# Storing output tile 58 as 104 + 24 rows instead of 100 + 28 rows

## The chip, the cores and the metric

The kernel runs on one core of one Trainium2 chip. The metric is the device time of one execution in microseconds (us). Before the change the median of the first three runs was 210.65 us (210.45 to 210.84).

## The reference

```python
batch, m, k, n = 16, 512, 1024, 768            # all float32
def reference(x, weight, bias, residual):
    return (np.matmul(x, weight) + bias + residual).astype(np.float32)
```

That is 8192 rows of 1024 numbers times a 1024x768 matrix. With `x` and the residual read and the output written, the core moves 87 MB.

## The kernel before

The 8192 rows are 64 tiles of 128 rows, in four superblocks S of 16 tiles. All loads and stores are issued on SyncE's queue in the fixed order of a list, `ORDER`. An entry `('s', S, j0, j1)` stores tiles `16*S+j0` to `16*S+j1-1`; a further number cuts the store's 128 partitions at that row into two stores. The end of the list is:

```python
ORDER = [ ...                                      # loads and earlier stores cut here
 ('r', 3, 7, 16), ('s', 2, 0, 16), ('s', 3, 0, 10), ('s', 3, 10, 11, 100), ('s', 3, 11, 13),
 ('s', 3, 13, 14), ('s', 3, 14, 15), ('c', 3, 15, 0), ('c', 3, 15, 1)]
LAST = [(0, 512), (512, 256)]                      # columns of the two stores of tile 63
```

So the program ends with these stores: ten tiles in one (48 to 57), tile 58 cut at row 100, tiles 59 and 60 in one, then 61, 62, and tile 63 in two column pieces. The issuing code is:

```python
n0, nl = (0, N) if kind == "s" else LAST[j1]
j1 = j1 if kind == "s" else j0 + 1
edges = [0, *cut, P]                               # P = 128
for p0, p1 in zip(edges, edges[1:]):
    K_(nc.sync.dma_start(
        out=out_d[S, p0:p1, j0:j1, n0:n0 + nl],
        in_=R[p0:p1, (J * S + j0) % RR:(J * S + j0) % RR + j1 - j0, n0:n0 + nl],
    ))
```

By the Trainium skill ("DMA: Bandwidth & Descriptors", section "Why a DMA increments its semaphore by 16 and not by 1"), a DMA issued from SyncE uses the largest k up to 16 that divides its number of rows, on the lowest-numbered k engines, and each of them increments the semaphore when its own share has landed. The trace agrees on k: the 100-row store has 10 completions, the 28-row store 14, and whole tiles have 16. Tile 58 is 128 rows of 3072 bytes, so the cut at 100 gives engines 0-9 ten rows and then two more, engines 10-13 two rows, and engines 14 and 15 none.

## Time and profile before

| | before |
|---|---|
| median of the first three runs | 210.65 us |
| span of the profiled run (its time: 210.74 us) | 209.0 us |
| end of the last vector add | 204.50 us |
| first and last of the 16 landings of the last store | 206.20 and 207.88 us |

From the page of before: busy time of TensorE, the tenths of busy time of PE and DMA in 40 slices of the span, and the DMA queues.

```profile
span 209.0 us, 3115 instructions
PE 201.5 (96%) x1298; PEld 130.0 (62%) x1298; DVE 104.7 (50%) x140; ACT 66.2 (32%) x69; POOL 115.9 (55%) x72
...
PE   7899999999999999999999999999999999999990
...
DMA  6999999999989899999999999999999999998984
...
q1 hardware_dynamic: 4912, 87.05, 97.9%
q8 instruction: 10, 0.16, 0.3%
```

TensorE and the DMA engines are both busy nearly all the time. For the tail the question is what ends last. From the chain that ended last, restricted to 201 us and later (start, duration, what):

```profile
200.79 0.65 PE psum_o L164 x4
201.44 2.61 PE psum_o L258 x16
204.05 0.02 issue
204.08 0.42 DVE ro L262
```

The computing is over at 204.50 us, 4.5 us before the span ends. From the waits of SyncE's queue from 190 us on (who waited for whom: us in total, times, longest):

```profile
SPq L292 <- DMA out_dram<-ro: 3.0, 1, 3.0
```

So the end is a wait for stores. From the table of stretches of before (stretch, its length, the busy time of the five engines, granted clock, DMA share, GB/s):

```profile
205.00:205.50 0.50, 0.00 (x0) 0.00 (x0) 0.00 (x0) 0.00 (x0) 0.00 (x0) 1.00 1.00 389
205.50:206.00 0.50, 0.00 (x0) 0.00 (x0) 0.00 (x0) 0.00 (x0) 0.00 (x0) 1.00 0.90 334
206.00:206.50 0.50, 0.00 (x0) 0.00 (x0) 0.00 (x0) 0.00 (x0) 0.00 (x0) 0.62 0.42 162
206.50:207.00 0.50, 0.00 (x0) 0.00 (x0) 0.00 (x0) 0.00 (x0) 0.00 (x0) 0.50 0.32 117
207.00:207.50 0.50, 0.00 (x0) 0.00 (x0) 0.00 (x0) 0.00 (x0) 0.00 (x0) 0.50 0.14 49
207.50:208.00 0.50, 0.00 (x0) 0.00 (x0) 0.00 (x0) 0.00 (x0) 0.00 (x0) 0.50 0.00 0
```

The second-to-last number is the one to read. The share is 1.00 while all 16 engines work, and then it falls, to 0.90, 0.42, 0.32 and 0.14. The engines do not finish together; a few carry a backlog. (A packet counts in the stretch in which it starts, and the last landing comes 0.34 us after the end of the last packet. So the share is 0.00 after 207.50 us although landings follow until 207.88.) The semaphore records of the trace say how many. The 16 landings of the last store (issued at 204.53 us), in us:

```
206.20 206.21 206.24 206.25 206.28 206.30 206.31 206.34 206.38 | 206.65 207.07 207.14 207.38 207.50 207.83 207.88
```

Nine engines land about 1.7 us after the issue. That is the latency of a small store on an idle engine. The other seven are still busy with earlier stores.

Two further readings need the packet records of the trace (start, duration and size of every DMA packet, without the engine's number). On one engine the next packet starts 3 or 4 ns before the previous one ends, and the sequence of sizes is known from `ORDER`. So the packets can be chained into 16 sequences, one for each engine. Where two engines start packets of the same size within about 2 ns the chains may be swapped; the packets of tile 58 show which group of engines a chain belongs to. A 3072-byte packet takes 121 ns and the next one starts 118 ns after it, so **one row of tile 58 costs its engine 0.118 us**.

The ten packets of queue 8 are instruction fetches of 16 KB each. The Trainium skill ("Runtime: NRT & Kernel Launch", section "Instruction fetch mechanics") says that instructions are refilled in 16 KiB blocks of 256. TensorE's 2 x 1298 instructions make just over ten such blocks, which agrees with the ten packets. That the fetches are TensorE's rests on this count; the trace does not name their engine. Each fetch sits in one engine's chain, between its data packets. This is one engine of 10-13 in the trace of before (start us, ns, bytes):

```
174.350  1029  27648
175.375  1033  27648
176.405  1098  16384   <- instruction fetch
177.488  1493  27648   <- the next packet takes 0.46 us longer as well
178.978     9      4   <- its completion
```

This engine loses about 1.55 us to the fetch: 1.08 us from the fetch's start to the next packet's, and 0.46 us in that packet. The fetch at 196.4 us does the same to an engine of 14-15, which loses 1.42 us (1.04 + 0.39). These two hits fall just before the end and are not made up for: at the end of the ten-tile store these two engines were at 202.57 and 202.40 us and all others between 198.8 and 201.1. Without the 1.55 us the first would have been near 201.0. That the fetches are the cause rests on this sum.

### The profile page before, as it was taken

Reading aid. Unit: us, or ns where it says so; the run is one execution under the profiler, and the core shown is the slowest. Engines: PE = TensorE matmul, PEld = TensorE weight load, DVE = VectorE, ACT = ScalarE, POOL = GpSimd, SP = SyncE. Lnnn points to the kernel's source line nnn. Section 1 sums busy time; section 2 is a strip of 40 time slices with the busy share of each in tenths; the row PEclk is TensorE's granted clock in tenths of the full one; section 3 lists DMA queues with packets and bytes.
Section 4 is the critical chain, followed back from the end, with each engine's and each line's share of the span. In section 5 each row is a group of like instructions: output and inputs, shape, how many; then the busy total and the mean of one; then the engine's idle time right before and its main releaser. Section 6 shows DMA issues by size and latency. Waiting matters only on the chain.

```text
span 209.0 us, 3115 instructions
## 1 busy us (share of the span) xinstructions
PE 201.5 (96%) x1298; PEld 130.0 (62%) x1298; DVE 104.7 (50%) x140; ACT 66.2 (32%) x69; POOL 115.9 (55%) x72
## 2 busy tenths in 40 slices
PE   7899999999999999999999999999999999999990
PEld 2455666666666666666666666666666666666660
DVE  0457555445545543654455454645545544654551
ACT  2444513312730372420370094320091056440000
POOL 2100029769999804999029702999108950699400
PEclk9999999999999999999999999999999999999997
DMA  6999999999989899999999999999999999998984
GB/s 238 427 426 436 423 430 455 400 459 418 466 379 496 384 395 431 453 414 417 425 460 441 415 429 458 433 408 423 425 471 419 416 425 473 442 442 372 432 360 186
DMA packets 4926, 87.24 MB, mean 417 GB/s; under 512 B 556, under 2 KB 684, under 8 KB 1840
## 3 DMA queue, kind: packets, MB, share of 16 engines
q1 hardware_dynamic: 4912, 87.05, 97.9%
q8 instruction: 10, 0.16, 0.3%
q14 instruction: 4, 0.03, 0.0%
HBM read 61.88 MB, written 25.17 MB: 417 GB/s over the span
## 4 chain that ended last, share of the span: by engine, by line
PE 92%; DMA 4%; ACT 1%; DVE 1%; SPq 0%; issue 0%
PE psum_o L164 78%; PE pt L157 13%; DMA x_tile<-in_x_dram 4%; PE psum_o L258 1%; ACT xb L146 1%; DVE xt L158 0%; DVE ro L262 0%; SPq L119 0%; SPq L122 0%
## 5 line engine op out<-in xcount | busy, mean ns | idle before, releaser
L164 PE MATMUL psum_o<-w_sb,xt 128*128 128x512 bf16 x1008 | 174.0, 326 | 0.5 <-DVE xt L158 0.3
L164 PEld LDWEIGHTS <-xt 128*128 128x128 bf16 x1008 | 98.5, 98 | 59.2 <-DVE xt L158 0.7
L189 POOL TENSOR_TENSOR ro<-ro,bias_sb 128x768 f32<-128x768 f32 x50 | 88.8, 1816 | 48.5 <-DMA ro<-in_residual_dram 38.0
L149 ACT CAST xb<-x_tile 128x1024 bf16<-128x1024 f32 x60 | 59.7, 1043 | 113.8 <-DMA x_tile<-in_x_dram 75.6
L158 DVE COPY xt<-pt 128x1024 bf16<-128x1024 bf16 x64 | 44.0, 690 | 83.3 <-PE pt L157 83.3
L199 DVE TENSOR_TENSOR ro<-psum_o,ro 128x768 f32<-128x768 f32 x49 | 46.5, 948 | 5.8 <-POOL ro L189 4.6
L157 PE MATMUL pt<-ident,xb 128*128 128x128 f32 x256 | 38.4, 274 | 0.9 <-DVE xb L149 0.7
L185 POOL TENSOR_TENSOR ro<-ro 128x768 f32<-128x768 f32 x14 | 25.0, 1819 | 25.1 <-DMA ro<-in_residual_dram 24.9
L157 PEld LDWEIGHTS pt<-ident,xb 128*128 128x128 f32 x256 | 29.6, 140 | 9.4 <-issue 1.1
L195 DVE TENSOR_TENSOR ro<-psum_o,bias_sb 128x768 f32<-128x768 f32 x14 | 13.2, 947 | 0.0
L208 PE MATMUL psum_o<-warm 128*128 128x512 bf16 x12 | 4.5, 554 | 1.2 <-DVE warm_a L204 1.2
L229 ACT CAST w_sb<-ro 128x768 bf16<-128x768 f32 x4 | 3.3, 832 | 3.7 <-DMA ro<-in_weight_dram 3.7
L229 POOL CAST w_sb<-ro 128x768 bf16<-128x768 f32 x1 | 0.8, 822 | 5.4 <-DMA ro<-in_weight_dram 5.4
L208 PEld LDWEIGHTS <-warm 128*128 128x128 bf16 x12 | 1.5, 135 | 3.7 <-issue 2.2
L149 DVE CAST xb<-x_tile 128x1024 bf16<-128x1024 f32 x1 | 0.7, 694 | 4.4 <-DMA x_tile<-in_x_dram 4.4
L146 ACT CAST xb<-x_tile 128x512 bf16<-128x512 f32 x3 | 1.8, 617 | 3.4 <-PE psum_o L164 1.7
L258 PE MATMUL psum_o<-w_sb,xt 128*128 128x512 bf16 (+1 forms) x16 | 2.8, 326 | 0.0
L229 DVE CAST w_sb<-ro 128x768 bf16<-128x768 f32 x3 | 1.7, 557 | 2.0 <-DMA ro<-in_weight_dram 2.0
L147 DVE CAST xb<-x_tile 128x512 bf16<-128x512 f32 x3 | 1.2, 424 | 2.6 <-DMA x_tile<-in_x_dram 2.6
L258 PEld LDWEIGHTS <-xt 128*128 128x128 bf16 x16 | 1.6, 98 | 1.1
L223 PE MATMUL psum_o<-warm 128*128 128x512 bf16 x6 | 1.6, 379 | 0.0
L262 DVE TENSOR_TENSOR ro<-psum_o,ro 128x512 f32<-128x512 f32 (+1 forms) x2 | 1.1, 558 | 0.9 <-PE psum_o L258 0.8
(14 smaller groups left out, 5.1 us busy)
## 6 DMA issues: line engine op xcount, KB each, us to landing
out_dram<-ro SPq DMA_DIRECT2D x3, 6144.0 KB, 34.6
x_tile<-in_x_dram SPq DMA_DIRECT2D x3, 5120.0 KB, 24.1
ro<-in_residual_dram SPq DMA_DIRECT2D x3, 3840.0 KB, 25.5
x_tile<-in_x_dram SPq DMA_DIRECT2D x3, 3072.0 KB, 40.7
ro<-in_residual_dram SPq DMA_DIRECT2D x3, 2304.0 KB, 17.5
x_tile<-in_x_dram SPq DMA_DIRECT2D x4, 1024.0 KB, 8.2
x_tile<-in_x_dram SPq DMA_DIRECT2D x2, 2048.0 KB, 21.0
out_dram<-ro SPq DMA_DIRECT2D x1, 3840.0 KB
```

The lines of the kernel that those rows point to most:

```text
L146: K_(nc.scalar.copy(out=dst[:, 0:K // 2], in_=src[:, 0:K // 2]))
L149: K_((nc.scalar.copy if how == "s" else nc.vector.tensor_copy)(out=dst, in_=src))
L157: K_(nc.tensor.transpose(out=pt[:, q, :], in_=words[:, ts(q, P)], identity=ident))
L158: K_(nc.vector.tensor_copy(out=XT[t % XT_N].rearrange("p q m e -> p (q m e)"), in_=pt.rearrange("p q m -> p (q m)").bitcast(BF16),))
L164: K_(nc.tensor.matmul(PO[t % HEAD][:, n0:n0 + nl], lhsT=XT[t % XT_N][:, q, :, e], rhs=w_sb[:, q, e, n0:n0 + nl], start=(q == 0 and e == 0) ...
L185: K_(nc.gpsimd.tensor_add(out=r, in0=r, in1=tmp(t)))
L189: K_(nc.gpsimd.tensor_add(out=r, in0=r, in1=bias_sb))
L195: K_(nc.vector.tensor_add(out=tmp(t), in0=p, in1=bias_sb))
L199: K_(nc.vector.tensor_add(out=row(t), in0=p, in1=row(t)))
L208: K_(nc.tensor.matmul(PO[0][:, 0:512], lhsT=warm[:, 0:P], rhs=warm, start=True, stop=True))
L229: K_(copy(out=w_sb[:, q, e, :], in_=w_st[:, 2 * q + e, :]))
L258: K_(nc.tensor.matmul(p, lhsT=XT[t % XT_N][:, q, :, e], rhs=w_sb[:, q, e, n0:n0 + nl], start=(q == 0 and e == 0), stop=(q == n_q - 1 and e ...
```

## The change

The intent is to take rows from engines that end late and give them to engines that have slack.

```diff
- ('r', 3, 7, 16), ('s', 2, 0, 16), ('s', 3, 0, 10), ('s', 3, 10, 11, 100), ('s', 3, 11, 13),
+ ('r', 3, 7, 16), ('s', 2, 0, 16), ('s', 3, 0, 10), ('s', 3, 10, 11, 104), ('s', 3, 11, 13),
```

Now 104 rows go to 13 engines (8 each) and 24 rows to 12 engines (2 each):

| rows of tile 58 on engine | 0-9 | 10, 11 | 12 | 13 | 14, 15 |
|---|---|---|---|---|---|
| before | 12 | 2 | 2 | 2 | 0 |
| changed | 10 | 10 | 8 | 0 | 0 |

The bytes, the number of DMAs and every instruction of the other engines stay the same.

## The prediction

> **What bounds the kernel now.** The page shows a span of 209.0 us with PE busy 96% and the DMA slices mostly at 9 tenths. The chain of waits ends with the last vector add at 204.50 us; the queue's waits show SyncE then waiting 3.0 us for a store, the longest wait of the end. The stretches from 204.5 us on show the DMA share falling: 1.00 (205.0-205.5), 0.42, 0.32, 0.14, 0 after 207.5. So the engines do not finish together: a few run late with a backlog.
>
> The trace's semaphore increments (one per engine and DMA) say how late. For the last store (128x256, issued at 204.53) nine engines land between 206.20 and 206.38 us, seven at 206.65, 207.08, 207.14, 207.38, 207.50, 207.83 and 207.88. The same seven are late in the stores before. So the span ends with the slowest engine's backlog, not with the last store's latency (1.7 us).
>
> **Which engines are late.** I followed each engine's packets by their back-to-back start times and sizes. By the Trainium skill ("DMA: Bandwidth & Descriptors", section on why a DMA increments its semaphore by 16), a DMA uses the largest k up to 16 that divides its rows, on the lowest-numbered k engines. The trace agrees on k: 10 completions for 100 rows, 14 for 28. So tile 58 now gives engines 0-9 12 rows each, 10-13 two, 14-15 none. By that: of the latest seven, five belong to 0-9, one (207.50) to 14-15, and the last of all (207.88) to 10-13. The last two classes are late because the ten 16 KB instruction fetches (about 1.05 us each, queue 8) fall on one engine after another; those at 176.4 and 196.4 us hit one engine of 10-13 and then one of 14-15. The order of the earlier hits (three in 0-9, three in 10-13) fits consecutive engines 7 to 14, so I take the two as 13 and 14. That is an inference; engine numbers are not in the trace.
>
> **What the change does.** The same bytes, DMAs and instructions. 104 rows go to engines 0-12 (8 each), 24 rows to 0-11 (2 each). Engines 0-9: 12 to 10 rows; 10-11: 2 to 10; 12: 2 to 8; 13: 2 to 0; 14-15 stay at 0. A 3072-byte packet takes 121 ns and repeats every 118 ns (packet records). So engines 0-9 and 13 end 0.24 us earlier, 10 and 11 0.94 us later, 12 0.71 us later. Engines 10-12 have slack: they are at 203.0-203.2 at the two-tile store where the last is at 205.07, so they would end near 206.9.
>
> **Sum.** 207.88 becomes 207.65 (engine 13), 207.83 becomes 207.60 (slowest of 0-9), engine 14 stays at 207.50. The last landing, hence the span, moves by -0.23 us, all of it on the path; PE is untouched. Predicted 210.4 us, range 210.1 to 210.85. Faster by over 2%: 0.5%; within 2%: 99%; slower: 0.5%.
>
> **Right or wrong in the profile.** Right: 13 and 12 completions for tile 58; last landing about 207.65 with a second just below; wait of SyncE at the end near 2.8 us; last vector add unchanged at 204.5. Wrong: if the fetched engine is 10, 11 or 12, the last landing goes to 208.6-208.8 and the time to about 211.4-211.6.
>
> **What would make it wrong.** The fetches may fall on other engines from run to run (the three times, 210.45-210.84, spread as much as the gain); the numbering inference may fail.

## The result, and the profile after

| | before | changed |
|---|---|---|
| median of 6 runs, same rounds | 210.56 us | 210.33 us |
| range | 210.45 to 210.84 | 210.12 to 210.52 |
| span of the profiled run | 209.0 us | 208.3 us |
| landings of the last store | 206.20 to 207.88 us | 206.18 to 207.25 us |

The ratio was 0.9988 with a 95% interval of 0.9975 to 1.0001: the same within 2%, and the interval just touches 1. Ratios here are the mean time of one kernel's fast runs over the mean of the other's of the same rounds, so they are not quite the ratios of the medians quoted.

From the page of the changed kernel:

```profile
span 208.3 us, 3115 instructions
PE 201.8 (97%) x1298; PEld 130.1 (62%) x1298; DVE 104.7 (50%) x140; ACT 66.1 (32%) x69; POOL 116.0 (56%) x72
...
DMA  6999999999989999999999999999999999999995
...
q1 hardware_dynamic: 4913, 87.05, 98.1%
q8 instruction: 10, 0.16, 0.3%
```

From its chain that ended last, from 201 us on, and from its waits of SyncE's queue from 190 us on:

```profile
200.80 0.65 PE psum_o L164 x4
201.45 2.61 PE psum_o L258 x16
204.07 0.02 issue
204.09 0.42 DVE ro L262
```

```profile
SPq L292 <- DMA out_dram<-ro: 2.4, 1, 2.4
```

The computing ends within 0.02 us of where it did. The last wait went from 3.0 to 2.4 us. From the table of stretches of the changed kernel:

```profile
205.00:205.50 0.50, 0.00 (x0) 0.00 (x0) 0.00 (x0) 0.00 (x0) 0.00 (x0) 1.00 0.98 381
205.50:206.00 0.50, 0.00 (x0) 0.00 (x0) 0.00 (x0) 0.00 (x0) 0.00 (x0) 1.00 0.96 354
206.00:206.50 0.50, 0.00 (x0) 0.00 (x0) 0.00 (x0) 0.00 (x0) 0.00 (x0) 1.00 0.43 156
206.50:207.00 0.50, 0.00 (x0) 0.00 (x0) 0.00 (x0) 0.00 (x0) 0.00 (x0) 0.82 0.13 43
207.00:207.50 0.50, 0.00 (x0) 0.00 (x0) 0.00 (x0) 0.00 (x0) 0.00 (x0) 0.50 0.00 0
```

The work that still stood at 0.14 after 207.0 us is gone. The completions are 13 and 12 for tile 58, as intended. The last landing is at 207.25 us instead of 207.88.

That is 0.63 us in this pair of profiles, nearly three times the predicted 0.24, while the medians differ by 0.23 only. The chains explain this. The engine with the fetch at 176 us finished its share of the ten-tile store, which comes *before* tile 58, at 202.57 us in the profile of before and at 202.15 us in that of the changed kernel. The two programs are identical up to there, so 0.42 us is spread from run to run. Between that point and the end of its share of tiles 59 and 60 it took 2.09 us before and 1.85 us after: 0.24 us less, which is its two rows. Its own last landing thus moved from 207.88 to 207.21 us. The last of all, 207.25, was then that of another engine, a slow one of 0-9 (see c1_stairs), which had landed at 207.83 before. The pair of profiles flatters the change: the execution profiled after (210.12 us) was the fastest of its six, and the one before (210.74 us) lay above the median of its kernel.

The chains also settle that engine's number. Before, it had two rows of the 28-row store and none of the 100-row store, so it is one of 10-13. After, it has nothing of tile 58, so it is not one of 0-12. Given the rule quoted from the skill, it is engine 13.

### The profile page after: what moved, and what is told of

The parts are those of the page before. It is cut to its first block, busy times and chain, and to the rows that moved or that the text cites. A ratio compares the mean times of both kernels' runs of the same rounds, so it can differ in the third digit from the quotient of the medians.

```text
span 208.3 us, 3115 instructions
## 1 busy us (share of the span) xinstructions
PE 201.8 (97%) x1298; PEld 130.1 (62%) x1298; DVE 104.7 (50%) x140; ACT 66.1 (32%) x69; POOL 116.0 (56%) x72
## 4 chain that ended last, share of the span: by engine, by line
PE 92%; DMA 4%; DVE 1%; SPq 0%; ACT 0%; issue 0%
PE psum_o L164 78%; PE pt L157 13%; DMA x_tile<-in_x_dram 4%; PE psum_o L258 1%; DVE xt L158 0%; ACT xb L146 0%; DVE ro L262 0%; SPq L119 0%; SPq L122 0%
```

## The experiments

Eleven kernels were run in three jobs, each beside runs of the kernel before on the same chip; each was correct. All edits are to the one entry for tile 58. In the column of rows, a dash means none.

| run | cut of tile 58 at rows | rows on 0-6 / 7-9 / 10-12 / 13 / 14 / 15 | median us (beside it: before) | ratio, 95% interval |
|---|---|---|---|---|
| a1_again | 104 (the change) | 10 / 10 / 10, 10, 8 / - / - / - | 210.26 (210.43) | 0.999 (0.9978-1.0003) |
| a2_whole | none | 8 / 8 / 8 / 8 / 8 / 8 | 211.19 (210.43) | 1.0035 (1.0022-1.0047) |
| a3_126 | 126 | 10 on 0, 1; else 9 / 9 / 9 / 9 / - / - | 211.06 (210.43) | 1.0035 (1.0022-1.0048) |
| a4_117 | 117 | 10 / 10 / 10, 9, 9 / - / - / - | 210.42 (210.43) | 0.9997 (0.9984-1.0011) |
| b1_24first | 24 | as the change | 210.68 (210.86) | 0.9994 (0.9982-1.0007) |
| b2_only13 | 100, 126 | 13 on 0, 1; else 12 / 12 / 2 / - / - / - | 210.68 (210.86) | 0.9992 (0.9978-1.0006) |
| c1_stairs | 49, 101, 111, 120 | 14 / 7, 6, 5 / 4 / - / - / - | 210.6 (210.86) | 0.999 (0.9977-1.0003) |
| b4_119 | 119 | 18 / 1, 1, 0 / - / - / - / - | 211.27 (210.86) | 1.003 (1.0017-1.0043) |
| d1_again | 104 (the change) | as the change | 210.4 (210.56) | 0.9996 (0.9982-1.0009) |
| d2_117 | 117 | as a4_117 | 210.23 (210.56) | 0.9984 (0.9972-0.9997) |
| d3_keep13 | 91, 100 | 10 / 10, 10, 9 / 9 / 2 / - / - | 210.36 (210.56) | 0.9992 (0.9979-1.0004) |

The theory: each engine is a queue of its own, the end is the latest engine's backlog, and only the rows on the late engines count. The rivals: the change does nothing; evenness of the split, or the number of stores, counts; the partitions or the numbers 104 and 24 count; one part of the change alone makes the gain.

### a1_again: the change once more

No edit.

> The changed kernel again, for a tighter figure. Theory (backlog of single engines: engine 13 and the slowest of 0-9 carry two 3072-byte rows less each, 0.118 us a row): ratio 0.9989, last landing about 0.24 us below the kernel before on average. Rival (the gain seen is only spread from run to run, the change does nothing): ratio 1.000.

Measured: 0.999 (0.9978 to 1.0003), and the mean of its five runs was 0.23 us below the mean of before. This fits the theory, but by its interval it does not exclude the rival.

### a2_whole: tile 58 in one store

```diff
- ('s', 3, 10, 11, 100)
+ ('s', 3, 10, 11)
```

> Tile 58 in one store, 8 rows on each of 16 engines. Theory: engine 13 gets six rows more than before (+0.71 us), engine 14 eight more (+0.94 from a lower start), 0-9 four less; last landing near 208.6, ratio 1.0034. Rival (an uneven split costs time, engines are alike): ratio below 1, about 0.998, as no engine has more than 8 rows and there is one store less.

Measured: 1.0035 (1.0022 to 1.0047), +0.71 us by the means. The even split is slower, as the theory has it, and the rival falls. From the table of stretches of this run:

```profile
206.50:207.00 0.50, 0.00 (x0) 0.00 (x0) 0.00 (x0) 0.00 (x0) 0.00 (x0) 1.00 0.15 57
207.00:207.50 0.50, 0.00 (x0) 0.00 (x0) 0.00 (x0) 0.00 (x0) 0.00 (x0) 1.00 0.13 49
207.50:208.00 0.50, 0.00 (x0) 0.00 (x0) 0.00 (x0) 0.00 (x0) 0.00 (x0) 1.00 0.09 31
```

One engine of 16 is a share of 0.06 and two are 0.13. Exactly two engines work from 207.0 us on. They are the two with the late fetches, and they land at 208.03 us (engine 13, with the fetch at 177.0 us) and 208.40 us (the one of 14-15, with the fetch at 196.4 us); the next before them lands at 207.20. Expected were 208.6 and 208.44, worked out from the profile of before. The engine of 14-15 came within 0.04 us of its figure and set the end. Engine 13 came 0.57 us early, because it ended its ten-tile share 0.55 us earlier than in the profile of before (202.02 us against 202.57).

### a3_126: nine rows on engine 13 as well

```diff
- ('s', 3, 10, 11, 100)
+ ('s', 3, 10, 11, 126)
```

> 126 rows on 14 engines (9 each), 2 rows on two engines. Engines 0-12 carry 9 or 10 rows, nearly as in the changed kernel; engine 13 carries 9 where it carries none there and two before. Theory: engine 13 ends 7 x 0.118 = 0.83 us later than before, last landing near 208.7, ratio 1.0039, and engine 13 alone stands out in the last landings. Rival (not engine 13 but the 0-9 ones set the end): as the changed kernel, ratio 0.999.

Measured: 1.0035 (1.0022 to 1.0048). From its table of stretches:

```profile
206.50:207.00 0.50, 0.00 (x0) 0.00 (x0) 0.00 (x0) 0.00 (x0) 0.00 (x0) 1.00 0.10 35
207.00:207.50 0.50, 0.00 (x0) 0.00 (x0) 0.00 (x0) 0.00 (x0) 0.00 (x0) 1.00 0.07 25
207.50:208.00 0.50, 0.00 (x0) 0.00 (x0) 0.00 (x0) 0.00 (x0) 0.00 (x0) 0.85 0.02 8
```

A share of 0.07 is one engine alone. This run also holds the cleanest comparison inside one profile: engine 13 and the engine of 14-15 with the late fetch ended their shares of the ten-tile store 0.02 us apart (201.89 and 201.87 us). Engine 13 then had nine rows of tile 58 and the other none, and their last landings are 208.03 and 206.96 us. The difference of 1.07 us is the nine rows at 0.118 us (1.06). The expected absolute landing, 208.7, was off, because engine 13 was 0.68 us less late before tile 58 than in the profile of before.

### a4_117 and d2_117: the change's loads with another cut

```diff
- ('s', 3, 10, 11, 100)
+ ('s', 3, 10, 11, 117)
```

> 117 rows on 13 engines (9 each), 11 rows on 11 engines (1 each): 0-10 carry 10 rows, 11 and 12 carry 9, 13-15 none. Theory: same as the changed kernel, ratio 0.9989; against the 126-row cut about 1.06 us less, though those two differ almost only in engine 13. Rival (row counts, alignment or the count 104/24 itself matter): differs from the changed kernel by over 0.2 us.

Measured: 0.9997 (0.9984 to 1.0011). Against the 126-row cut it is 0.64 us less by the medians, not the 1.06 expected. The 1.06 was engine 13's own difference, and the end falls only until the next late engine is last. In this profile one of 0-9 landed last, at 207.47 us, and engine 13 at 207.12. The mean was 0.14 us above a1_again, less than the 0.2 us set for the rival, but enough to try again:

> The 117-row cut again: engines 0-10, 13, 14 and 15 carry exactly what they carry in the changed kernel, 11 has one row less and 12 one more, both with slack. The first time its mean was 0.09 us below the kernel before, 0.14 us worse than the changed kernel. Theory (rows on the late engines alone count): within 0.08 us of the changed kernel of this job, ratio 0.999. Rival (the 104/24 split has something of its own, such as its partitions or store shapes): again 0.1 us or more worse.

Measured: 0.9984 (0.9972 to 0.9997), the best interval of all, and this time its mean was 0.25 us *below* that of the changed kernel of its job, where at most 0.08 us of difference was expected. That expectation was missed. So a first difference of 0.14 us one way and a second of 0.25 us the other way came from programs with the same loads on every late engine. That is the size of difference that two kernels can show here for no cause in the change. Neither sign can be read as a property of the 104/24 cut.

### d1_again: the change a third time

> The changed kernel a third time. Theory: mean 0.24 us below the kernel before (so far 0.26 and 0.23), ratio 0.9989. Rival (no effect): 1.000.

Measured: 0.9996 (0.9982 to 1.0009). Its five runs were 210.16 to 210.54 and one of 211.0. The mean was 0.10 us below before. Taken together, the 16 runs of the changed kernel in three jobs lie 0.20 us below the mean of before of their own job (0.26, 0.23 and 0.10), and the ten runs of the 117-row cut lie 0.22 us below it. With b1_24first (below) that makes six comparisons of kernels that store tile 58 in two pieces and relieve both engine 13 and engines 0-9. All six lie below before, by 0.09 to 0.35 us. This speaks against the rival that nothing happens, though only one interval of the six, that of d2_117, leaves out 1.

### b1_24first: other partitions, the same loads

```diff
- ('s', 3, 10, 11, 100)
+ ('s', 3, 10, 11, 24)
```

> The same loads on every engine as in the changed kernel, but the first 24 rows go in the 12-engine store and the last 104 in the 13-engine store, so every engine reads other partitions. Theory (only the number of rows on each engine counts): as the changed kernel, ratio 0.999, last landings of engine 13, of engine 14 and of one of 0-9 within 0.1 to 0.2 us of each other. Rival (which partitions an engine reads matters): ratio off by over 0.002.

Measured: 0.9994 (0.9982 to 1.0007). This is within the 0.002 that was set, so no effect of the partitions was seen; one under 0.2 us would not have been. The last four landings were 207.49, 207.62, 207.69 and 207.91 us. The very last was one of the low-numbered engines, with two smaller fetches of 8 KB. Engine 13 (207.69), the one of 14-15 (207.62) and this one lie 0.29 us apart, more than the 0.1 to 0.2 us expected.

### b2_only13 and d3_keep13: the two halves

b2_only13 takes engine 13's two rows away and leaves 0-9 nearly as they were; d3_keep13 relieves 0-9 and leaves engine 13 its two rows.

```diff
- ('s', 3, 10, 11, 100)
+ ('s', 3, 10, 11, 100, 126)
```

> Pieces of 100, 26 and 2 rows: engine 13 is relieved of its two rows as in the change, but engines 2-9 keep 12 rows and 0-1 get 13. Theory: engine 13 ends 0.24 us earlier, yet the slow one of 0-9 (it lands 0.05 us before engine 13 in the profile of before) then sets the end: gain near 0.05 us, ratio 0.9998; in the trace the last landing is of the engine with the 12 or 13 rows and the long 0.46 us from last packet to landing. Rival (engine 13 alone set the end): as the changed kernel, ratio 0.999.

Measured: 0.9992 (0.9978 to 1.0006). The expectation of the trace failed: engine 13 landed last all the same (207.89 us), because in this run it finished the ten-tile store at 202.82 us, 0.25 us later than in the profile of before. The engine of 14-15 landed just before it (207.87), and the slow engine of the low-numbered ones at 207.62.

```diff
- ('s', 3, 10, 11, 100)
+ ('s', 3, 10, 11, 91, 100)
```

> Pieces of 91, 9 and 28 rows: engines 0-8 carry 10 and 9 carries 9, as in the change, but engine 13 keeps its two rows (10-12 carry 9, 14 and 15 none). The half of the change that relieves 0-9, alone. Theory: engine 13 ends where it ended before and nearly always sets the end: gain 0.03 us, ratio 0.9998; in the trace the last landing is engine 13's, with its two rows of the 28-row store. Rival (the relief of 0-9 is the gain): ratio 0.999.

Measured: 0.9992 (0.9979 to 1.0004). The expectation of the trace held: the last landing (207.82 us) follows from the last completion of the 28-row store (203.19 us, where all others were done by 202.66). That engine, the one with the fetch at 176.4 us, has its completion of the ten-tile store at 202.96 us and added two rows, 0.235 us, with nothing of the 91-row store. Two rows and no more is the load of engine 13 alone in this cut, so it is engine 13. The time decided nothing, as both theory (0.9998) and rival (0.999) lie in the interval. **How the gain divides between the two halves stays open.** Each half gave 0.16 to 0.19 us by the means and the whole 0.20, but none of these differs from the others by more than the repeats of one and the same load do. Both halves also have a third store, and that alone shortens the time by 0.06 us, as the next part shows.

### c1_stairs and b4_119: which of the engines 0-9 is the other slow one

In every profile that could be followed, one chain of 0-9 was late though it had no 16 KB fetch. Its packets in the large stores are longer than those of all others: in the profile of before, its 16 tiles of superblock 2 took 0.58 us more than eight packets of the usual 1.815 us, which is 4%. Its loads are as fast as those of the others, and its completion of the last store takes about 0.45 us from packet to semaphore where the others take about 0.34. A staircase of rows tells its number:

```diff
- ('s', 3, 10, 11, 100)
+ ('s', 3, 10, 11, 49, 101, 111, 120)
```

> Pieces of 49, 52, 10, 9 and 8 rows: 14 rows on each of 0-6, 7 on engine 7, 6 on 8, 5 on 9, 4 on 10-12, none on 13-15. The number of its packets thus tells which engine of 0-9 is the slow one. Theory: it is engine 7, with 7 packets; it then ends 0.59 us earlier than before and leaves the last three, engine 13 ends 0.24 us earlier, and one of 0-3 with two small instruction fetches comes up by 0.24 us and ties with 13: last landing near 207.6 against 207.9 in the profile of before, ratio 0.999. Rival (the slow engine is one of 0-6, 14 packets): it ends 0.24 us later than before, near 208.1, ratio 1.001.

Measured: 0.999 (0.9977 to 1.0003). The slow chain has 14 packets of tile 58, not 7. So it is one of 0-6, and the guess of engine 7 was wrong. Engine 7, known by its seven packets, was among the earliest and had no fetch, and so was engine 8. The rival's number, 1.001, was wrong too: the slow engine, engine 13 and two more all landed between 207.67 and 207.89 us.

The time gained 0.21 us by the means, but in the profile this is not a gain of the DMA engines: the last landing, 207.89 us, is where it was before. What became shorter is the time after it, 0.89 us to the end of the span against 1.09 before. The instruction records show why. At the end SyncE checks the semaphores of the stores in a fixed order, one every 0.06 us. With two pieces of tile 58 the last store's semaphore is in the first check and four more follow its landing; with five pieces it is in the fourth check and one more follows. With three pieces (b2_only13 and d3_keep13) it is in the second check, and the time after the last landing was 1.03 and 1.02 us. So **the number of stores does count a little**, by where the last store falls in SyncE's checks. It does not touch the comparison of before and changed, which both have two pieces (1.09 us each). The packet count decided here; the time did not.

```diff
- ('s', 3, 10, 11, 100)
+ ('s', 3, 10, 11, 119)
```

> 119 rows on seven engines (17 each), 9 rows on nine: 18 rows on 0-6, 1 on 7 and 8, none on 9-15. Theory with the slow engine at 7: it drops out of the last ones (11 rows less, -1.3 us); the end is set by one of 0-3, 0.71 us later than before, near 208.1: ratio 1.001, 1.002 at most. Rival (slow engine among 0-6): near 208.5, ratio 1.003 or more. Rival (engines 0-9 have slack and 13 alone counts): as the changed kernel, 0.999.

Measured: 1.003 (1.0017 to 1.0043), +0.63 us by the means, as the rival with the slow engine among 0-6 had it. It lands last, at 208.41 us, after three others at 208.00 to 208.06, and it has rows of both pieces (17 + 1), so it is again one of 0-6. So several of engines 0-6 have no slack for six more rows; c1_stairs showed engines 7 and 8 early. The change took its room from 10-12.

### The sum that holds in all runs

For engine 13 the landing of the last store can be written as the time at which it ends its share of the ten-tile store, plus 0.118 us for each of its rows of tile 58, plus a rest. From the packet and semaphore records:

| profile | end of its ten-tile share | rows of tile 58 | its last landing | rest |
|---|---|---|---|---|
| before | 202.57 | 2 | 207.88 | 5.07 |
| after | 202.15 | 0 | 207.21 | 5.06 |
| a1_again | 202.32 | 0 | 207.38 | 5.06 |
| a2_whole | 202.02 | 8 | 208.03 | 5.07 |
| a3_126 | 201.89 | 9 | 208.03 | 5.08 |
| a4_117 | 202.04 | 0 | 207.12 | 5.08 |
| b1_24first | 202.63 | 0 | 207.69 | 5.06 |
| b2_only13 | 202.82 | 0 | 207.89 | 5.07 |
| b4_119 | 202.62 | 0 | 207.69 | 5.07 |
| c1_stairs | 202.61 | 0 | 207.67 | 5.06 |
| d1_again | 202.54 | 0 | 207.61 | 5.07 |
| d2_117 | 202.07 | 0 | 207.14 | 5.07 |
| d3_keep13 | 202.51 | 2 | 207.82 | 5.07 |

The rest is 5.07 us within 0.02. So in these profiles the rows act exactly as costed, and the spread is all in the second column, a point that the change does not touch: 0.93 us from the least to the greatest. It falls into two groups. In the five profiles where the fetch came at 177.0 to 177.1 us, among the packets of superblock 2's store, the second column is 201.89 to 202.15. In the eight where it came at 176.2 to 176.7 us, among those of the load before it, it is 202.32 to 202.82. Why the fetch falls now here and now there, no run shows. The profile of before is one of the eight and that of the changed kernel one of the five.

The time of a run is its last landing plus about 2.87 us (210.74 and 207.88 before, 210.12 and 207.25 after, 211.28 and 208.40 for a2_whole), save that with three and five pieces it is 2.83 and 2.71 us for the reason given at c1_stairs. The last landing is a maximum over several engines.

## Why the prediction was right or wrong

- **What bounds the kernel: right.** The end is the backlog of single engines. a2_whole and a3_126 put rows on the two engines named, and exactly those two, or that one, then stand out in the last stretches. In a2_whole the last of all was the engine of 14-15, which got eight rows, as its own sum (208.44 against 208.40 measured) had it.
- **Cost of a row: right.** 0.118 us a row, within 0.02 us over zero to nine rows.
- **Engine 13: right, and shown by the traces, given the skill's rule of which engines a store uses.** By the groups that its packets fall into before and after, the engine with the fetch at 176 us can only be 13; d3_keep13 shows it within one profile. That the other is 14 rather than 15 no run shows, since no cut here separates those two.
- **"The order of the earlier hits ... fits consecutive engines 7 to 14": wrong as far as the chains can be trusted.** In the chains of c1_stairs engines 7 and 8 have no 16 KB fetch, and two of 0-6 have one; those of b4_119 say the same. (These chains reach back some 140 us, where swaps are possible.) The conclusion held because engine 13's place did not depend on it.
- **Slack of 10-12: right.** With eight and six rows more they did not come last in any profile that could be followed. In the profile of after the last three engines were the slow one of 0-6, 13 and the one of 14-15.
- **The size: right on average.** Predicted -0.24 us on the path. The trace shows exactly that for engine 13, the medians of the first measurement gave -0.23, and 16 runs in three jobs gave -0.20. Part of this closeness is luck: the three jobs gave 0.26, 0.23 and 0.10, and programs with the same loads on the late engines differed by 0.14 and 0.25 us. The range given, 210.1 to 210.85 us, also holds the time of before, so the measured time by itself says little for the mechanism. What speaks for it is the sum above and a2_whole and a3_126.
- **The landing of the profiled run: off by 0.40 us.** Predicted 207.65, measured 207.25; and the wait of SyncE was 2.4 us instead of 2.8. The term mis-sized was the starting point: I took engine 13's lateness from one profile as if it were a constant. It lay at 202.57 us there and between 201.89 and 202.82 in the others of the table.
- **The tie at the end: only partly foreseen.** I named engine 13, the slowest of 0-9 and the one of 14-15 as the next to bind. In the profiles after they land within 0.1 to 0.4 us of each other and take turns: the slow one of 0-6 was last in the profile of after, the one of 14-15 in d1_again, engine 13 in b2_only13. In b1_24first a fourth was last, the one with the two 8 KB fetches, which I had not named. That is why the halves of the change cannot be told apart by the clock.

As an estimate from these landings: 13 and 14 have no rows of tile 58 left, and moving rows of other tiles off them would put these on 0-12, among them the slow engine of 0-6 that already ties with them. The cut at 104 is thus, by this estimate, near the best that a cut of tile 58 alone can give, and no experiment pointed to a version clearly better than both.

## What to carry to other kernels

When the last stores finish, look at how the DMA share falls: a share of one or two sixteenths means one or two engines with a backlog, and then the question is which engine is late and how many bytes it has yet to move, not how fast the last store is. A store's row count decides how many engines carry it, so a cut of one late store is a cheap way to move bytes from late engines to those with slack; an even split was the slower one here by 0.7 us. A gain of a tenth of a per cent should be read as a difference between two marks on one engine's chain in the trace, since the starting point of that chain moved by 0.9 us from run to run, nearly four times the gain. And when the number of stores changes, look also at the time after the last landing: here it moved by up to 0.2 us for a reason that has nothing to do with the backlog.

## What the Trainium skill lacked or had wrong

- "Runtime: NRT & Kernel Launch", section "Instruction fetch mechanics", says that the cost of crossing a 16 KiB boundary is one DMA tail-bump, mostly hidden. It is hidden from TensorE here (busy all of 175 to 180 and of 195 to 200 us), but not from the DMA engine that carries the block: in two hits that were followed, the engine lost 1.55 and 1.42 us of data movement (1.08 and 1.04 us for the fetch, 0.46 and 0.39 us in the packet after it). In this kernel that helps to set which engine ends last. No page has it.
- "CRC Debugging", section "Comparing the Two Runs", gives queue 14 as that of the sequencers' instruction refills. Here ten packets of 16 KB were on queue 8, and in the span four of 8 KB on queue 14.
- "DMA: Bandwidth & Descriptors", section "Latency and other measured facts", calls engines 7 and 15 usually slower, which by its best guess is tied to DMAs issued from GpSimd. With all data moved by SyncE's queue, engine 7 was among the earliest in the one run that identifies it, which does not go against that guess. Instead one engine of 0-6 was slow, in stores alone: 4% longer packets and 0.1 us more from packet to semaphore, in every profile that could be followed. No page has that.
- The same page has no trn2 figure for what a store on fewer than 16 engines costs the issuing queue when it follows another such store at once. The first of two such stores took 0.31 to 0.35 us to issue and each further one 1.06 to 1.25 us (five pieces in c1_stairs: 0.31, 1.07, 1.23, 1.20, 1.21 us). It cost nothing here, since SyncE had time; what the longer ones wait for was not tried.
